# Rotary over two token tiles, padded GLA queries copied by ScalarE, and the second layer's convolution norm in borrowed memory

## The chip, the cores and the metric

The kernel runs on one core of one Trainium2 chip. A core has TensorE (PE in the profile, with its weight loads as PEld), VectorE (DVE), ScalarE (ACT), GpSimd (POOL) and SyncE (SP), which issues the DMAs. Each engine works through its own list of instructions in order, and waits on semaphores for the others. The metric is the device time of one execution, in microseconds (us), and its median over several runs.

## The reference: what is computed

Two layers of a mixer for a diffusion generator, in float32: 1024 latent tokens and 256 context tokens of width 1024. Each layer projects the normalised input once, and feeds three branches; a gate multiplies each branch, and one output projection joins them.

```python
pl = _project(hl, w_in); pc = _project(hc, w_in)        # hc: the context's h; layer 1 needs only k, v and decay of it
# A: convolution of width 31 over the tokens, then a norm over the 256 channels, then silu
u = conv(a_val * sigmoid(a_glu)) + conv_b
u = ((u - mean(u)) * rsqrt(var(u) + eps) * ln_w + ln_b);  a = silu(u) * silu(a_gate)
# B: windowed attention; q (8 heads) and k (2 heads) of 64 get a rotary on the latent tokens
rot = concat([-x[..., 32:], x[..., :32]]);  x = x * cos + rot * sin
# C: bidirectional gated linear attention (GLA), 4 heads, dk 32, dv 64, chunks of 64 tokens
q_in = q * exp(b);  k_in = k * exp(-b)                  # b: cumulative log decay in a chunk
att = where(causal, q_in @ k_in, 0);  o = att @ v + q_in @ S
S = decay * S + (k * exp(b_last - b)) @ v               # the state, from chunk to chunk
```

## The kernel before, in words

Tokens are columns in some stages and rows in others, in tiles of 128: ten tiles, 0 and 1 being the context. h lies transposed in three chunks: c=0 (context, 256 tokens, tile `HC`, 4096 columns), c=1 and c=2 (512 latent tokens each, tiles `H1`, `H2`). A float32 product is made of three passes over high and low parts (`three`, line 673), so PE's bulk is `ps<-WS,H` (weights stationary), or `ps<-H,WS` (tokens stationary).

The order of the instructions is made by a planner. Each piece of work is a generator (a lane) with a priority; `loop` (line 201) goes on with the ready lane of the best priority, where ready is judged by clocks of the engines that `Model` (line 49) keeps from a cost formula. The lists it writes are then fixed. Every instruction is recorded through a helper (line 43), so that all rows of the profile show L43; one goes by tiles. `SM` are 14 small slots of 512 columns, `WR` slots for raw weights and for scratch, `ps` the banks of PSUM, `mix` the wide tiles in which the branches' values stand.

`phase_a` (line 1571) runs a layer's input projection group by group, in the order of `GROUPS` (line 1735): convolution input (0, 1), GLA's v (10), GLA's q and k (8), attention's k and v (5), its q (3, 4), the convolution's gate (2), GLA's gate (9), attention's gates (6, 7). PE fills a PSUM bank by 48 or 96 matmuls, ACT copies it out (`SM<-ps 128x512`), and the bank is free again. Beside these groups run lanes:

- `ev_qk_b` (line 898) takes a pair of token tiles of groups 5, 3 or 4: ACT copies the bank to an `SM` slot, POOL applies `rope` (line 886) to each of the two tiles of a latent pair, and a DMA stores the pair. A pair of k and v has 2 heads of k to turn, a pair of q 4 heads. There are 8 pairs of k and v and 16 of q in both layers.
- `gla_states` (line 1059), one lane for each direction d: DVE forms b_last - b, ACT its exp, POOL multiplies by k (`SM<-SM,mix`), PE transposes the product (`ps<-idr,SM`) and multiplies it by v, DVE steps the state S. POOL's list holds these products between the rotaries.
- `gla_out` (line 1121), one call for each of 10 token tiles in layer 0 and 8 in layer 1, two lanes in parallel: ACT makes exp(b/16) and exp(-b/16) of both directions, the products with q and k follow, PE multiplies the two (`ps<-SM,SM 128*64 128x256`, the score matmuls), DVE applies the causal mask, PE sums, and a norm follows. q goes into `qx`, padded tiles in which head h of the 128 rows has its own block and zeros elsewhere, hence four products of 32x128.
- `conv_taps` (line 924): 62 DVE instructions a layer (`mix<-U,small,mix`, 128x1295 or 128x1024), placed wherever the planner finds DVE free for 0.3 us.
- `conv_ln` (line 939), the norm over channels of a chunk: PE transposes, DVE statistics, PE transposes back, ACT and DVE finish. It takes `SM` slots. In layer 1 one lane does c=1 and then c=2.
- `attn_start` (line 1186) opens the attention. It uses `HC`'s memory for its keys' and queries' tiles, which the flag `hcfree1` guards in layer 1.

Of the kernel before, what the change touches and what calls it, by code (L numbers as in the profile page):

```python
# [164 lines left out]
class Hybrid:  # L165
# [124 lines left out]
    def mix_new(self, dt):  # L290

        t, old = self.tile("mix4", 4 * TC, dt), self.mixes[1]
        m, b = self.nc.part(t)
        m[1, b] = self.nc.touched(old) if old is not None else 0.0
        self.mixes[1] = t
        return t

    def mix(self, a, t, p=slice(None)):
# [584 lines left out]
                self.flag(f"v{l}.{i}")  # L883
        return ev

    def rope(self, x, nh, blk, tmp):

        nc = self.nc
        x4 = x.rearrange("p (h a b) -> p h a b", a=2, b=32)
        t4 = tmp.rearrange("p (h a b) -> p h a b", a=2, b=32)  # L890
        cos, sin = [self.rt[:, s * 256 + blk * 32:s * 256 + blk * 32 + 32][:, None, None, :].to_broadcast([128, nh, 2, 32]) for s in range(2)]
        e = nc.gpsimd
        e.tensor_tensor(t4, x4[:, :, ::-1, :], sin, op=ALU.mult)
        e.tensor_tensor(x4, x4, cos, op=ALU.mult)
        e.tensor_tensor(x4[:, :, 0], x4[:, :, 0], t4[:, :, 0], op=ALU.subtract)
        e.tensor_tensor(x4[:, :, 1], x4[:, :, 1], t4[:, :, 1], op=ALU.add)

    def ev_qk_b(self, l, name, dst, nh):

        def ev(i0, p):  # L900
            nc = self.nc
            yield self.need("SM"), self.need("WR", 1, 1), f"rope{l}"
            s, tmp = self.sm(512), self.get("WR")
            s3 = s.rearrange("p (s c) -> p s c", s=2)
            nc.scalar.activation(s3, p, ACTF.Copy)
            yield
            if i0 >= 2:
                for r in range(2):
                    self.rope(s3[:, r, 0:nh * 64], nh, i0 + r - 2, tmp[:, r * 256:r * 256 + nh * 64])
            self.free(tmp)  # L910
            yield
            nc.sync.dma_start(dst[i0:i0 + 2].rearrange("s p c -> p s c"), s3)
            self.free(s)
            for i in (i0, i0 + 1):
                self.flag(f"{name}{l}.{i}")
        return ev
# [19 lines left out]
                    nc.vector.scalar_tensor_tensor(acc, src, self.p_conv_w(l, j, s), acc, op0=ALU.mult, op1=ALU.add)  # L936
        self.flag(f"conv{l}")

    def conv_ln(self, l, c):
        nc = self.nc  # L940
        t0, n = CH[c]
        nt = n // 128
        yield self.need("SM", (nt + 1) // 2, 2)
        xs = [self.sm(512).rearrange("p (q x) -> p q x", q=2) for _ in range((nt + 1) // 2)]
        for q0 in range(0, nt, 2):
            yield self.bank_need("tr")
            tp = self.bank_get("tr")
            for q in (q0, q0 + 1):
                o = col(t0) + q * 128
                for j in range(2):  # L950
                    nc.tensor.transpose(tp[:, (q - q0) * 256 + j * 128:(q - q0) * 256 + (j + 1) * 128],
                                        self.mix(j, slice(o, o + 128)), self.idf)
            yield
            mv = self.ti(4).rearrange("p (q x) -> p q x", q=2)
            for r in range(2):
                bs = self.bst[:, q0 + r]
                nc.vector.bn_stats(bs, tp[:, r * 256:(r + 1) * 256])
                nc.vector.bn_aggr(mv[:, r], bs)
            rs = self.rstd(mv[:, :, 1], 1.0, 2)
            yield  # L960
            for r in range(2):
                nc.vector.tensor_scalar(xs[q0 // 2][:, r], tp[:, r * 256:(r + 1) * 256], mv[:, r, 0:1], rs[:, r:r + 1],
                                        op0=ALU.subtract, op1=ALU.mult)
            self.free(tp)
        yield
        for j in range(2):
            yield self.bank_need("tr")
            bk = self.bank_get("tr")
            for q in range(nt):
                nc.tensor.transpose(bk[:, q * 128:(q + 1) * 128], xs[q // 2][:, q % 2, j * 128:(j + 1) * 128], self.idf)  # L970
            yield None, self.need("SM", 2), f"ag{l}.0.{c}", f"ag{l}.1.{c}"
            ys, ts = self.sm(512), self.sm(512)
# [9 lines left out]
            self.free(ys, ts)  # L982
        self.free(*xs)
        self.flag(f"ln{l}{c}")


# [134 lines left out]
    def gla_out(self, l, i, qx, v):  # L1121
        nc = self.nc
        o = col(i * 128)
        yield self.need("SM", 2), self.rest(v), f"T{l}.0.{self.hslot(i)[0]}"
        self.load_vz(i, v)
        ws, A = self.sm(512), self.sm(512)
        w = ws.rearrange("p (a t) -> p a t", a=4)
        for d in range(2):
            b = self.mix(4 + d, slice(o, o + 128))
            nc.scalar.activation(w[:, d], b, ACTF.Exp, scale=1.0 / 16.0)  # L1130
            nc.scalar.activation(w[:, 2 + d], b, ACTF.Exp, scale=-1.0 / 16.0)
        yield self.at(ws)
        for d in range(2):
            nc.gpsimd.tensor_tensor(w[:, 2 + d], w[:, 2 + d], self.mix(3, slice(o, o + 128)), op=ALU.mult)
            for h in range(4):
                r = slice(32 * h, 32 * h + 32)
                nc.vector.tensor_tensor(qx[d][r, h], w[r, d], self.mix(2, slice(o, o + 128), r), op=ALU.mult)
        yield None, self.bank_need("tr")
        at = self.bank_get("tr")
        for d in range(2):  # L1140
# [34 lines left out]
        tp = self.bank_get("tr")  # L1175
# [395 lines left out]
    def phase_a(self, l):  # L1571
# [9 lines left out]
        for g in GROUPS[:-1]:  # L1581
# [25 lines left out]
            elif g == 2:  # L1607
                yield from self.t_group(l, g, self.ev_agate(l), cx)

                def ln():  # L1610
                    for c in range(1 if l else 0, 3):
                        yield from self.conv_ln(l, c)
                self.go(ln(), 3)
            elif g == 9:
                yield from self.t_group(l, g, self.ev_mgate(l, 6), cx)
            else:
                self.cap.update(mm=2, tr=CAPB[0], ac=CAPB[1])
                self.cap["md"] = 0 if l else MDC
# [216 lines left out]
```

## Time and profile before

| | |
|---|---|
| median of 3 runs | 1350.08 us (1346.76 to 1352.33) |
| the profiled execution | 1350.69 us, its span 1348.9 us |
| mean granted TensorE clock | 0.977 |
| PE / DVE / ACT / POOL busy | 1253.7 / 962.9 / 560.2 / 542.9 us |
| instructions of PE / DVE / ACT / POOL | 9198 / 1856 / 1251 / 769 |

Layer 0's projection groups from the convolution's input to GLA's gate lie before 330 us, those of layer 1 between about 790 and 1068 us, the attentions behind them. A row of a timeline shows the start, the duration, the engine, the operation with its tiles and shapes, how many alike were joined (x), and in brackets the idle time ahead of it with what ended it.

### The profile page before, as it was taken

How to read it: one execution, taken by the hardware profiler on the slowest of the kernel's cores; microseconds unless marked ns; L12 is line 12 of the kernel's file. 1: busy time of each engine (PE TensorE's matmuls, PEld its weight loads, DVE VectorE, ACT ScalarE, POOL GpSimd, SP SyncE). 2: the span in 40 equal slices, each digit the busy share in tenths (PEclk: the TensorE clock that was granted, in tenths of full speed). 3: DMA queues.
4: the chain of work that ended last, by engine and by line, in shares of the span. 5: the costliest groups of instructions: out<-in, count | busy, mean ns of one | idle time of the engine just before them, and what ended most of it. 6: DMA issues, size and time to landing. Idle time of an engine off the chain costs nothing. (4 is left out here: it accounts for less than half of the span.)

```text
span 1348.9 us, 24464 instructions
## 1 busy us (share of the span) xinstructions
PE 1253.7 (93%) x9198; PEld 1089.8 (81%) x9198; DVE 962.9 (71%) x1856; ACT 560.2 (42%) x1251; POOL 542.9 (40%) x769
## 2 busy tenths in 40 slices
PE   5999997889999999899999889988899999999997
PEld 3678886778788777779988879977787888898997
DVE  5835894888556577777776676896966478887864
ACT  3711431112223456456652461341112256676751
POOL 1410065956223334434341132056792335645430
PEclk9999988999999999899999989989999999999999
DMA  9453113222114333432113441113232113311112
GB/s 328 143 151 102 47 32 99 59 73 74 29 32 126 120 102 106 137 106 67 48 40 110 139 168 56 53 40 104 69 81 54 39 43 102 98 44 52 63 36 79
DMA packets 113239, 116.48 MB, mean 86 GB/s; under 512 B 38464, under 2 KB 81760, under 8 KB 113120
## 3 DMA queue, kind: packets, MB, share of 16 engines
q1 hardware_dynamic: 113120, 114.92, 28.2%
q8 instruction: 72, 1.18, 0.4%
q14 instruction: 47, 0.39, 0.1%
HBM read 95.47 MB, written 19.42 MB: 85 GB/s over the span
## 5 line engine op out<-in xcount | busy, mean ns | idle before, releaser
L43 PE MATMUL ps<-H,WS 128*128 128x512 f32 x1344 | 339.1, 399 | 3.6 <-ACT U L43 1.7
L43 PEld LDWEIGHTS ps<-H,WS 128*128 128x128 f32 x1344 | 245.1, 189 | 64.2 <-issue 10.0
L43 PE MATMUL ps<-WS,H 128*128 128x256 f32 x1704 | 258.3, 294 | 8.1 <-DVE H L43 4.7
L43 ACT ACTIVATE SM<-ps 128x512 f32<-128x512 f32 (+3 forms) x180 | 92.6, 517 | 397.8 <-PE ps L43 284.2
L43 PEld LDWEIGHTS ps<-WS,H 128*128 128x128 f32 x1704 | 232.1, 198 | 21.4 <-issue 10.2
L43 PE MATMUL ps<-idr,SM 128*128 128x128 f32 (+1 forms) x1076 | 150.5, 273 | 38.1 <-POOL SM L43 25.5
L43 DVE SCALAR_TENSOR_TENSOR mix<-U,small,mix 128x1295 f32<-128x1295 f32 (+1 forms) x120 | 177.6, 1526 | 0.2
L43 PEld LDWEIGHTS ps<-idr,SM 128*128 128x128 f32 (+1 forms) x1076 | 124.1, 143 | 62.2 <-POOL SM L43 29.6
L43 DVE SCALAR_TENSOR_TENSOR H<-ps,H 128x512 fp32r<-128x512 f32 x160 | 105.7, 681 | 46.3 <-ACT H L43 46.1
L43 ACT ACTIVATE SM<-SM,stat 128x641 f32<-128x641 f32 (+2 forms) x144 | 110.5, 769 | 56.4 <-DVE stat L43 43.0
L43 ACT ACTIVATE H<-ps 128x512 fp32r<-128x512 f32 x176 | 99.4, 597 | 80.5 <-PE ps L43 73.9
L43 POOL TENSOR_TENSOR SM<-SM,SM 128x256 f32<-128x256 f32 (+4 forms) x91 | 72.8, 808 | 149.0 <-ACT SM L43 112.5
L43 POOL TENSOR_TENSOR tir<-tir,mhalf 128x1 f32<-128x1 f32 (+2 forms) x55 | 44.9, 820 | 197.8 <-DVE tir L43 173.4
L43 DVE CUSTOM_DVE_ANT_0 SM<-ps,SM,small 128x640 f32<-128x640 f32 (+2 forms) x128 | 102.3, 809 | 25.5 <-PE ps L43 24.7
L43 POOL TENSOR_TENSOR SM<-SM,WR 128x128 f32<-128x128 f32 (+2 forms) x117 | 90.8, 793 | 21.4 <-DVE SM L43 14.2
L43 PE MATMUL ps<-H,H 128*128 128x256 f32 x552 | 97.5, 286 | 0.0
L43 PE MATMUL ps<-H 128*128 128x512 f32 x320 | 97.0, 409 | 0.2 <-DVE H L43 0.2
L43 PE MATMUL ps<-SM,SM 128*32 128x128 f32 (+4 forms) x764 | 81.3, 295 | 12.5 <-DVE SM L43 7.8
L43 PEld LDWEIGHTS ps<-H,H 128*128 128x128 f32 x552 | 81.6, 189 | 1.4 <-issue 0.4
L43 POOL TENSOR_SCALAR SM<-SM,tir 128x640 f32<-128x640 f32 (+2 forms) x77 | 67.7, 892 | 28.5 <-DVE tir L43 18.0
L43 PE MATMUL ps<-WS,SM 128*128 128x256 f32 x248 | 70.2, 283 | 0.0
L43 PE MATMUL ps<-H,SM 128*128 128x256 f32 x248 | 69.4, 280 | 0.0
(150 smaller groups left out, 2121.9 us busy)
## 6 DMA issues: line engine op xcount, KB each, us to landing
WR<-in_w_in_dram SPq DMA_DIRECT2D x80, 256.0 KB, 3.9
WR<-in_w_mod_dram SPq DMA_DIRECT2D x64, 256.0 KB, 3.1
WR<-in_w_out_dram SPq DMA_DIRECT2D x32, 256.0 KB, 3.4
SM<-vd SPq DMA_DIRECT2D x116, 64.0 KB, 2.4
x<-SM SPq DMA_DIRECT2D x20, 256.0 KB, 2.3
SM<-x SPq DMA_DIRECT2D x20, 256.0 KB, 4.3
qd<-SM SPq DMA_DIRECT2D x18, 256.0 KB, 2.2
mix<-in_x_dram SPq DMA_DIRECT2D x8, 512.0 KB, 8.3
```

Source lines behind the costliest of these rows:

```text
L43: r = getattr(self._e, op)(*a, **k)
```

## The change

1. `rope` takes both token tiles of a pair at once, in five POOL instructions instead of two times four: the sine products of either half (two), the cosine product over everything, the subtraction and the addition.
2. `gla_out`: ACT's four exps of 128x128 become two of 128x256; the products with q and with k are two DVE instructions of 128x256 (before: eight of 32x128 on DVE, two of 128x128 on POOL); eight new ACT copies of 32x128 then carry q into the padded `qx`.
3. Layer 1's `conv_ln` works in the memory of `HC` (the context's h, which is no longer needed by then), as two lanes of priority 3, one for a chunk; `hcfree1` is given at their end, and `attn_start` of layer 1 waits for it.

```diff
-    def rope(self, x, nh, blk, tmp):
...
-        e.tensor_tensor(t4, x4[:, :, ::-1, :], sin, op=ALU.mult)
-        e.tensor_tensor(x4, x4, cos, op=ALU.mult)
-        e.tensor_tensor(x4[:, :, 0], x4[:, :, 0], t4[:, :, 0], op=ALU.subtract)
-        e.tensor_tensor(x4[:, :, 1], x4[:, :, 1], t4[:, :, 1], op=ALU.add)
+    def rope(self, x, t, nh, blk):
...
+        for a in range(2):
+            e.tensor_tensor(t5[:, :, :, a], x5[:, :, :, 1 - a], sin.to_broadcast([128, 2, nh, 32]), op=ALU.mult)
+        x4 = x.rearrange("p s (g b) -> p s g b", b=32)
+        e.tensor_tensor(x4, x4, cos.to_broadcast([128, 2, 2 * nh, 32]), op=ALU.mult)
+        for a, op in ((0, ALU.subtract), (1, ALU.add)):
+            e.tensor_tensor(x5[:, :, :, a], x5[:, :, :, a], t5[:, :, :, a], op=op)
...
-    def conv_ln(self, l, c):
+    def conv_ln(self, l, c, own=None):
...
+            xs = [own[:, 512 * q:512 * q + 512] for q in range(2)]
+            yield self.rest(own)
...
+        both = self.mix(slice(4, 6), slice(o, o + 128))
+        for a in range(2):
+            nc.scalar.activation(w[:, 2 * a:2 * a + 2], both, ACTF.Exp, scale=(1.0 - 2 * a) / 16.0)
+        yield self.at(ws)
+        for a in range(2):
+            nc.vector.tensor_tensor(w[:, 2 * a:2 * a + 2], w[:, 2 * a:2 * a + 2],
+                                    self.mix(2 + a, slice(o, o + 128))[:, None, :].to_broadcast([128, 2, 128]), op=ALU.mult)
+        yield
         for d in range(2):
-            b = self.mix(4 + d, slice(o, o + 128))
-            nc.scalar.activation(w[:, d], b, ACTF.Exp, scale=1.0 / 16.0)
-            nc.scalar.activation(w[:, 2 + d], b, ACTF.Exp, scale=-1.0 / 16.0)
-        yield self.at(ws)
-        for d in range(2):
-            nc.gpsimd.tensor_tensor(w[:, 2 + d], w[:, 2 + d], self.mix(3, slice(o, o + 128)), op=ALU.mult)
             for h in range(4):
                 r = slice(32 * h, 32 * h + 32)
-                nc.vector.tensor_tensor(qx[d][r, h], w[r, d], self.mix(2, slice(o, o + 128), r), op=ALU.mult)
+                nc.scalar.activation(qx[d][r, h], w[r, d], ACTF.Copy)
...
+        if l:
+            yield f"hcfree{l}"
...
+                def ln1():
+                    hc = self.hc_new(F32)
+                    yield tuple([self.go(self.conv_ln(l, c, hc[:, (c - 1) * 2048:c * 2048]), LNP) for c in (1, 2)])
+                    self.hc_new(F32R)
+                    self.flag(f"hcfree{l}")
+                self.go(ln1() if l else ln(), LNP if l else 3)
...
-                if l:
-                    self.flag(f"hcfree{l}")
```

POOL's list in layer 0, at the second pair of k and v, before the change. `SM2_271` holds the pair, `SM14` the cosines and sines, `WR0_272` the scratch; `SM8_266` and `SM5_268` are the products with k for the states of chunk 1, both directions:

```order
L43 TENSOR_TENSOR WR0_272_1795<-SM2_271_1794,SM14_1_65 128x128
L43 TENSOR_TENSOR SM2_271_1794<-SM2_271_1794,SM14_1_65 128x128
L43 TENSOR_TENSOR SM2_271_1794<-SM2_271_1794,WR0_272_1795 128x2x32 x2
L43 TENSOR_TENSOR WR0_272_1795<-SM2_271_1794,SM14_1_65 128x128
L43 TENSOR_TENSOR SM2_271_1794<-SM2_271_1794,SM14_1_65 128x128
L43 TENSOR_TENSOR SM2_271_1794<-SM2_271_1794,WR0_272_1795 128x2x32 x2
L43 TENSOR_TENSOR SM8_266_1758<-SM8_266_1758,mix_64 128x512
L43 TENSOR_TENSOR SM5_268_1766<-SM5_268_1766,mix_64 128x512
```

The same place of POOL's list after the change:

```order
L43 TENSOR_TENSOR SM8_266_1738<-SM8_266_1738,mix_64 128x512
L43 TENSOR_TENSOR WR0_272_1794<-SM2_271_1793,SM14_1_65 128x2x2x32 x2
L43 TENSOR_TENSOR SM2_271_1793<-SM2_271_1793,SM14_1_65 128x2x128
L43 TENSOR_TENSOR SM2_271_1793<-SM2_271_1793,WR0_272_1794 128x2x2x32 x2
L43 TENSOR_TENSOR SM5_268_1763<-SM5_268_1763,mix_64 128x512
```

The first product moved ahead of the second pair's rotary, the second one is behind it as before, and the rotary has five instructions instead of eight. In the same way both products of chunk 2 (`SM8_276`, `SM5_281`) now stand ahead of the first rotary of q, where before the second of them stood behind it.

PE's list at the same place, before: the transposes of the two products, among the matmuls of attention's k and v on the context's and the latent tokens (`WS1_191`):

```order
L43 MATMUL ps0_66<-WS1_191_1029,H2_0_104_491 128x256 x12
L43 MATMUL ps0_66<-WS1_191_1029,H2_1_105_492 128x256 x12
L43 MATMUL ps0_66<-WS1_191_1029,H2_0_104_491 128x256 x12
L43 MATMUL ps0_66<-WS1_191_1029,H2_1_105_492 128x256 x12
L43 MATMUL ps1_67<-WS1_191_1029,H2_0_104_491 128x256 x12
L43 MATMUL ps2_68<-idr_81,SM8_266_1758 128x128 x4
L43 MATMUL ps1_67<-WS1_191_1029,H2_1_105_492 128x256 x12
L43 MATMUL ps3_69<-idr_81,SM5_268_1766 128x128 x4
```

And after:

```order
L43 MATMUL ps0_66<-WS1_191_1029,H2_0_104_491 128x256 x12
L43 MATMUL ps2_68<-idr_81,SM8_266_1738 128x128 x4
L43 MATMUL ps0_66<-WS1_191_1029,H2_1_105_492 128x256 x12
L43 MATMUL ps3_69<-SM10_182_1013,SM3_267_1739 32x128 x4
L43 MATMUL ps0_66<-WS1_191_1029,H2_0_104_491 128x256 x12
L43 MATMUL ps3_69<-SM11_183_1014,SM3_267_1739 32x128 x4
L43 MATMUL ps0_66<-WS1_191_1029,H2_1_105_492 128x256 x12
L43 MATMUL ps4_70<-idr_81,SM5_268_1763 128x128 x4
```

The first transposes moved ahead by 48 matmuls, and the second ones by 24 (of the 128x256 kind).

ACT's list at the first two calls of `gla_out` in layer 0, before (`SM3_309` and `SM2_311` hold their exps, `mix4` the decay):

```order
L43 ACTIVATE SM5_302_2310<-ps0_66 128x512
L43 ACTIVATE SM6_305_2403<-ps3_69 128x512
L43 ACTIVATE SM3_309_2428<-mix4_222_1355 128x128 x4
L43 ACTIVATE SM2_311_2458<-mix4_222_1355 128x128 x4
L43 ACTIVATE SM8_310_2429<-ps3_69 128x256
L43 ACTIVATE SM6_322_2602<-ps1_67 128x512
```

And after, where `SM12` to `SM1` are the padded queries:

```order
L43 ACTIVATE SM5_302_2320<-ps1_67 128x512
L43 ACTIVATE SM3_306_2330<-mix4_222_1355 128x256 x2
L43 ACTIVATE SM6_308_2351<-mix4_222_1355 128x256 x2
L43 ACTIVATE SM12_244_1554<-SM3_306_2330 32x128 x4
L43 ACTIVATE SM9_245_1555<-SM3_306_2330 32x128 x4
L43 ACTIVATE SM0_246_1556<-SM6_308_2351 32x128 x4
L43 ACTIVATE SM1_247_1557<-SM6_308_2351 32x128 x4
L43 ACTIVATE SM5_311_2423<-ps0_66 128x512
L43 ACTIVATE SM2_307_2331<-ps4_70 128x256
```

Sixteen copies that wait for DVE's products now stand between the exps and the next copy of a filled bank, `SM5_311<-ps0_66`.

More of the change, by code (lines that the diff above doesn't have):

```diff
@@ L295, in mix_new, with hc_new @@
         self.mixes[1] = t
+        return t
+    def hc_new(self, dt):
+        t, old = self.tile("HC", 4096, dt), self.HC
+        m, b = self.nc.part(t)
+        m[1, b] = self.nc.touched(old)
+        self.HC = t
         return t
@@ L884, in ev_v @@
         return ev
-    def rope(self, x, nh, blk, tmp):
[L888 to L892, printed above, removed]
-        e.tensor_tensor(t4, x4[:, :, ::-1, :], sin, op=ALU.mult)
-        e.tensor_tensor(x4, x4, cos, op=ALU.mult)
-        e.tensor_tensor(x4[:, :, 0], x4[:, :, 0], t4[:, :, 0], op=ALU.subtract)
-        e.tensor_tensor(x4[:, :, 1], x4[:, :, 1], t4[:, :, 1], op=ALU.add)
+    def rope(self, x, t, nh, blk):
+        e = self.nc.gpsimd
+        cos, sin = [self.rt[:, s * 256 + blk * 32:s * 256 + blk * 32 + 64].rearrange("p (r b) -> p r b", b=32)[:, :, None, :] for s in range(2)]
+        x5, t5 = [z.rearrange("p s (h a b) -> p s h a b", a=2, b=32) for z in (x, t)]
+        for a in range(2):
[4 more added lines that the diff above has]
+            e.tensor_tensor(x5[:, :, :, a], x5[:, :, :, a], t5[:, :, :, a], op=op)
     def ev_qk_b(self, l, name, dst, nh):
@@ L907, in ev @@
             if i0 >= 2:
-                for r in range(2):
-                    self.rope(s3[:, r, 0:nh * 64], nh, i0 + r - 2, tmp[:, r * 256:r * 256 + nh * 64])
+                self.rope(s3[:, :, 0:nh * 64], tmp.rearrange("p (s c) -> p s c", s=2)[:, :, 0:nh * 64], nh, i0 - 2)
             self.free(tmp)
@@ L942, in conv_ln @@
         nt = n // 128
-        yield self.need("SM", (nt + 1) // 2, 2)
-        xs = [self.sm(512).rearrange("p (q x) -> p q x", q=2) for _ in range((nt + 1) // 2)]
+        if own is None:
+            yield self.need("SM", (nt + 1) // 2, 2)
+            xs = [self.sm(512) for _ in range((nt + 1) // 2)]
+        else:
+            xs = [own[:, 512 * q:512 * q + 512] for q in range(2)]
+            yield self.rest(own)
+        x3 = [x.rearrange("p (q x) -> p q x", q=2) for x in xs]
         for q0 in range(0, nt, 2):
@@ L961, in conv_ln @@
             for r in range(2):
-                nc.vector.tensor_scalar(xs[q0 // 2][:, r], tp[:, r * 256:(r + 1) * 256], mv[:, r, 0:1], rs[:, r:r + 1],
+                nc.vector.tensor_scalar(x3[q0 // 2][:, r], tp[:, r * 256:(r + 1) * 256], mv[:, r, 0:1], rs[:, r:r + 1],
                                         op0=ALU.subtract, op1=ALU.mult)
@@ L969, in conv_ln @@
             for q in range(nt):
-                nc.tensor.transpose(bk[:, q * 128:(q + 1) * 128], xs[q // 2][:, q % 2, j * 128:(j + 1) * 128], self.idf)
-            yield None, self.need("SM", 2), f"ag{l}.0.{c}", f"ag{l}.1.{c}"
-            ys, ts = self.sm(512), self.sm(512)
+                nc.tensor.transpose(bk[:, q * 128:(q + 1) * 128], x3[q // 2][:, q % 2, j * 128:(j + 1) * 128], self.idf)
+            yield None, (self.need("SM", 2) if own is None else 0.0), f"ag{l}.0.{c}", f"ag{l}.1.{c}"
+            ys, ts = (self.sm(512), self.sm(512)) if own is None else (own[:, 1024:1536], own[:, 1536:2048])
             y, t = ys[:, 0:n], ts[:, 0:n]
@@ L981, in conv_ln @@
                                            op0=ALU.mult, op1=ALU.mult)
-            self.free(ys, ts)
-        self.free(*xs)
+            if own is None:
+                self.free(ys, ts)
+        if own is None:
+            self.free(*xs)
         self.flag(f"ln{l}{c}")
@@ L1610, in ln @@
                 def ln():
-                    for c in range(1 if l else 0, 3):
+                    for c in range(3):
                         yield from self.conv_ln(l, c)
-                self.go(ln(), 3)
+                def ln1():
[4 more added lines that the diff above has]
+                self.go(ln1() if l else ln(), LNP if l else 3)
             elif g == 9:
@@ L1626, in phase_a @@
                         self.flag("mods")
-                    if p == 7:
+                    if p == 7 and (c or l == 0):
                         self.flag({0: f"hcfree{l}", 1: f"h1out{l}", 2: f"h2out{l}"}[c])
@@ L1732, in run @@
             self.loop(self.go(self.program(), 9))
+LNP = 3
 GROUPS = [0, 1, 10, 8, 5, 3, 4, 2, 9, 6, 7]
```

## The prediction

> **What bounds the kernel now.** I read the page's first part, then the waits of PE, the busy time by stretches, and at last the timelines of PE and POOL around PE's longest idle times. PE's busy time and the list of what it waited for (us in total, times, longest):
>
> ```profile
> PE 1253.7 (93%) x9198; PEld 1089.8 (81%) x9198; DVE 962.9 (71%) x1856; ACT 560.2 (42%) x1251; POOL 542.9 (40%) x769
> ```
>
> ```profile
> PE ps L43 <- POOL SM L43: 26.4, 14, 8.7
> PE ps L43 <- DVE SM L43: 15.2, 16, 2.0
> ```
>
> PE works 1253.7 of 1348.9 us, so the 95 us in which it stands still are nearly all there is to gain while its matmuls stay the same. The first two kinds of wait, 26.4 and 15.2 us, are those that the rotary's and GLA's edits can reach. Where they lie, by stretches (PE, PEld, DVE, ACT, POOL, granted clock):
>
> ```profile
> 178.00:330.00 152.00, 129.80 (x1188) 116.36 (x1187) 117.44 (x168) 28.19 (x77) 103.49 (x126) 0.91 0.26 68
> 330.00:500.00 170.00, 168.41 (x1188) 137.28 (x1188) 104.56 (x249) 62.49 (x141) 53.66 (x86) 1.00 0.28 83
> 880.00:1000.00 120.00, 107.33 (x969) 97.24 (x969) 97.33 (x139) 28.66 (x64) 83.31 (x106) 0.97 0.26 70
> 1068.00:1120.00 52.00, 50.41 (x287) 42.18 (x286) 40.91 (x101) 27.17 (x59) 22.17 (x41) 1.00 0.23 62
> ```
>
> Layer 0's GLA and rotary stage (178 to 330) leaves PE idle for 22.2 us and its clock at 0.91; layer 1's (880 to 1000) for 12.7 us. Right behind layer 0's stage PE is busy for 168.4 of 170 us: nothing there swallows time that is won earlier, so a gain in the stage reaches the end. The waits one by one, as PE's rows show them:
>
> ```profile
> 212.52 1.12 PE L43 MATMUL ps<-idr,SM 128*128 128x128 f32 x4 [8.68 <-POOL SM L43]
> ...
> 250.87 0.66 PE L43 MATMUL ps<-idr,SM 128*128 128x128 f32 x4 [4.09 <-POOL SM L43]
> ...
> 252.62 2.73 PE L43 MATMUL ps<-WS,H 128*128 128x256 f32 x12
> ...
> 255.63 1.69 PE L43 MATMUL ps<-WS,H 128*128 128x256 f32 x12
> ...
> 278.18 0.33 PE L43 MATMUL ps<-SM,SM 128*64 128x64 f32 x2 [0.95 <-DVE SM L43]
> ...
> 298.82 0.65 PE L43 MATMUL ps<-SM,SM 128*64 128x256 f32 x4 [1.87 <-DVE SM L43]
> 301.35 1.12 PE L43 MATMUL ps<-SM,SM 128*64 128x256 f32 x4 [1.87 <-DVE SM L43]
> 302.40 2.93 PE L43 MATMUL ps<-WS,H 128*128 128x256 f32 x12
> ...
> 918.30 0.66 PE L43 MATMUL ps<-idr,SM 128*128 128x128 f32 x4 [2.96 <-POOL SM L43]
> ```
>
> **The rotary in front of GLA's states.** The 8.68 us come about in POOL's list: the second pair of k and v is turned, and only then come the products with k that PE transposes.
>
> ```profile
> 197.49 1.27 POOL L43 TENSOR_TENSOR WR<-SM,SM 128x128 f32<-128x128 f32 x1 [4.49 <-ACT SM L43]
> 198.84 1.60 POOL L43 TENSOR_TENSOR SM<-SM,SM 128x128 f32<-128x128 f32 x1
> 200.52 3.02 POOL L43 TENSOR_TENSOR SM<-SM,WR 128x64 f32<-128x64 f32 x2
> ...
> 209.94 3.75 POOL L43 TENSOR_TENSOR SM<-SM,mix 128x512 f32<-128x512 f32 x2
> 213.66 0.45 POOL L43 TENSOR_TENSOR WR<-SM,SM 128x128 f32<-128x128 f32 x1
> ...
> 214.72 0.60 POOL L43 TENSOR_TENSOR SM<-SM,WR 128x64 f32<-128x64 f32 x2
> ...
> 236.26 1.29 POOL L43 TENSOR_TENSOR SM<-SM,mix 128x512 f32<-128x512 f32 x1
> ...
> 243.08 1.89 POOL L43 TENSOR_TENSOR SM<-SM,SM 128x256 f32<-128x256 f32 x1
> ...
> 248.29 2.52 POOL L43 TENSOR_TENSOR SM<-SM,mix 128x512 f32<-128x512 f32 x1
> ```
>
> ```profile
> 195.40 15.94 DVE L43 SCALAR_TENSOR_TENSOR mix<-U,small,mix 128x1295 f32<-128x1295 f32 x10
> ```
>
> From 197.49 to 209.94 the eight instructions take 12.45 us, about 1.6 us each; the same shapes take 0.3 to 0.45 us from 213.66 on, after DVE's ten taps of 1.6 us have ended (195.40 + 15.94). Beside the taps POOL gets through about one instruction a tap, whatever its size. So it is the count that costs: five instead of eight. I take four of 1.6 us, and 2.0 for the longer cosine product (256 elements beside taps: 1.9 in the row 243.08), 8.4 us, so the rotary ends at 205.9.
>
> The first product leaves this queue altogether: its exp is done when POOL falls idle for the 4.49 us ahead of 197.49,
>
> ```profile
> 193.59 0.63 ACT L43 ACTIVATE SM<-SM 128x512 f32<-128x512 f32 x1 [7.03 <-DVE SM L43]
> ```
>
> so it runs from 194.3 to at most 196.9 (2.52 us beside taps, row 248.29). PE's transposes of it stand 48 matmuls earlier; at 1.69 us for 12 (row 255.63) that is 6.8 us before 203.84, where PE's wait began, or 197.1: no wait. The second product ends at 205.9 + 2.5 = 208.4; PE comes to it at about 203.0 (36 matmuls and three short groups after 197.1). It waits 5.4 us there, in place of 8.68: **-3.3 us**. If the taps are thinner there, the product runs in 1.29 and the rotary in 6, and 7 of the 8.68 go; if the queue is as slow as before, nothing goes.
>
> The 4.09 us before 250.87 come from the same pattern, the first rotary of q (the row 243.08 is part of it) between the first product of chunk 2 at 236.26 and the second at 248.29.
>
> Both products now stand ahead of the q rotaries, so the second would run behind the first, from 237.6, far before 246.78, where this wait began: **-4.1 us**. What is late next is the state chain itself, since PE's transposes moved forward too; I count that under the new waits. Behind this gap, and behind the pair of 1.87 us gaps, the clock was halved:
>
> ```profile
> 299.50:306.20 6.70, 4.85 (x25) 3.90 (x26) 6.57 (x11) 0.00 (x0) 1.47 (x3) 0.50 0.20 59
> ```
>
> Behind 250.87 twelve matmuls took 2.73 us instead of 1.69: **-1.0 us**. Behind 299.5, 4.85 us of work ran at clock 0.50, and half of it is **-2.4 us**. The stretch behind the 8.68 us keeps its halved clock in my sum, since 5.4 us remain.
>
> The Trainium skill, page "TensorE: Matmul & The Clock Gate", section "Part 1", lets the clock fall only after an idle window of about 3.4 us. No gap as long stood before 299.5, where the trace has 0.50; by that rule the 2.4 us wouldn't hang on these gaps, and the gain would be 2.4 us less. The trace decides.
>
> **The queries by ScalarE.** What DVE does for one `gla_out` now, and what ACT's 128x128 exps and DVE's 128x256 products cost:
>
> ```profile
> 290.01 4.52 DVE L43 TENSOR_TENSOR SM<-SM,mix 32x128 f32<-32x128 f32 x8
> ...
> 296.05 5.15 DVE L43 TENSOR_TENSOR SM<-SM,mix 32x128 f32<-32x128 f32 x8
> ...
> 277.70 0.43 DVE L43 TENSOR_TENSOR SM<-SM 128x256 f32<-128x256 f32 x1
> ...
> 287.06 0.91 ACT L43 ACTIVATE SM<-mix 128x128 f32<-128x128 f32 x4
> ```
>
> Before, PE waits for eight products, 4.5 to 5.2 us. After, for two products of 0.43 and eight copies; four exps of 128 elements take 0.91, so a copy of 128 about 0.23 and eight 1.8: 2.7 us in all, 1.8 to 2.5 us less than before. That covers both gaps of 1.87: **-3.7 us**. The 0.95 at 278.18 is the mask's step behind taps, and stays. ACT pays eight copies, 1.8 us, less two exps, about 0.3, for each of 18 tiles: some 27 us on an engine that is busy for 28 of 152 us in the stage; not on the path. Bounds: the copies could cost what a bank's copy of 512 costs, 0.6 each, 4.8 us in all, and then both gaps stay.
>
> The Trainium skill speaks against the move: "ScalarE: Activation LUTs", section "Rules for kernel authors", budgets about 0.3 us an ACTIVATE plus 0.83 ns an element. That would be an estimated 3.2 us for eight copies, and the gain would be about 2 us less. The row above has less, 0.23 each in a series.
>
> **Layer 1.** The wait of 2.96 stands behind the same kind of rotary:
>
> ```profile
> 908.93 0.70 POOL L43 TENSOR_TENSOR WR<-SM,SM 128x128 f32<-128x128 f32 x1 [2.71 <-ACT SM L43]
> ...
> 916.99 1.26 POOL L43 TENSOR_TENSOR SM<-SM,mix 128x512 f32<-128x512 f32 x1
> ```
>
> Eight instructions in 8.06 us; five of them would be 5.0 us by count: 3.0 us off, I take **-2.5**. GLA's outputs there wait in two short gaps:
>
> ```profile
> 967.44 1.82 PE L43 MATMUL ps<-SM,SM 128*64 128x256 f32 x12 [0.92 <-POOL SM L43]
> 969.95 0.65 PE L43 MATMUL ps<-SM,SM 128*64 128x256 f32 x4 [0.70 <-DVE SM L43]
> ```
>
> **-1.6 us** if both go. The norm of the convolution lies in 1068 to 1120, where PE idles for 1.6 of 52 us: moving its DVE and ACT work out of the attention's start can win 1.6 at most, I take **-0.5**. Its transposes cost PE the same wherever they stand. Its DVE and ACT work moves beside GLA's gate group, under whose matmuls it hides: they fill PE for 67.6 of 68 us.
>
> ```profile
> 1000.00:1068.00 68.00, 67.58 (x531) 53.53 (x530) 37.79 (x93) 16.06 (x49) 25.48 (x35) 1.00 0.22 55
> ```
>
> **New waits.** The planner put PE's transposes and score matmuls earlier by 24 to 84 matmuls (3 to 12 us), as if the engines kept its times, which POOL beside taps does not. Estimate: three waits of about 1 us, as the 0.95 and 0.92 above, **+3.0**; bounds 0 and 8.7 (the longest wait comes back whole).
>
> **Sum:** -3.3 - 4.1 - 1.0 - 2.4 - 3.7 - 2.5 - 1.6 - 0.5 + 3.0 = -16.1. From the profiled 1350.7, which is 0.6 above the median, that makes **1334.6 us**. All bounds at their good end: 3.7 more on the first rotary, 2.4 of its halved clock, 3.0 without new waits, 1.1 on the norm, 0.5 on layer 1: 1323.9.
>
> **Rivals.**
> 1. *More than the sum.* The first wait goes nearly whole and no new ones come: 1324, with 1318 if the order also closes the small gaps elsewhere that the 95 us still contain. For it: taps thin out while the state chain waits. Chance 0.17.
> 2. *No change.* POOL's pace is set by taps and PE's list was moved forward by as much as POOL became faster; the waits come back under other names: 8.7 of new waits in place of 3.0, the gaps before GLA's outputs (3.7 and 1.6) and the halved clock behind them (2.4). Sum -16.1 + 5.7 + 5.3 + 2.4 = -2.7: 1348. For it: the planner's clock is PE's and it fills to the edge. Against it: two of the gaps are waits behind whole rotaries that no longer stand there. Chance 0.17.
> 3. *Slower, by ACT's queue.* The copies wait for DVE's products, which stand behind taps of 1.6 us, and behind the copies ACT's next bank copy waits, without which PE gets no bank. A bank takes PE 5.92 us to fill:
>
> ```profile
> 264.55 5.92 PE L43 MATMUL ps<-WS,HC 128*128 128x256 f32 x48
> ```
>
> With two banks the copy may be late by that. It is only lost when DVE has more than about three taps ahead of the products (3 x 1.6 + 0.9 + 1.8 = 7.5 for one tile, 3.6 more for the second tile of a pair). If each of nine pairs of tiles lost 1.5 us, and 1.2 of clock behind it, that is +24.3, and 1334.6 becomes 1358.9. Against it: between the products at 290.01 and at 296.05 there was room for one tap alone, and ACT is idle four fifths of the stage. Chance 0.09. The wait of `attn_start` for the norm is no rival of its own: the norm starts a whole group, 68 us by the row above, ahead of it.
>
> **How the numbers follow.** Chances: forecast 0.57, rivals 0.17, 0.17 and 0.09. The range 1319 to 1350 covers the forecast, most of rival 1 and rival 2. A measurement of this kernel tells 0.5% (6.8 us) from no change: faster is below 1343.9, slower above 1357.5. Faster: 0.56 of the forecast, rival 1, and 0.02 of rival 2, together 0.75. Same: the rest of the forecast and of rival 2, 0.16. Slower: rival 3, 0.09.
>
> **What would show it.** Right: in POOL's timeline near 197 to 206 five rotary instructions of about 1.6 us; PE's wait for the first product gone, and one of about 5 us for the second; no wait of 4 us before q's first pair; clock 1.00 where the scores of layer 0's outputs stand; POOL's waits at PE down from 26.4 to under 15 us, DVE's by 5. Wrong: PE waiting for ACT's `SM` or for banks in 250 to 330 and 960 to 1000; a stage 178 to 330 that is as long as before; or an idle stretch at the start of layer 1's attention.

## The result, and the profile after

The changed kernel takes 1332.84 us (median; 1331.86 to 1335.86), beside 1348.42 us for the kernel before on the same chip (1345.08 to 1352.33): a ratio of 0.9887, 95% interval 0.9854 to 0.9921. Measured again later it took 1333.13, ratio 0.9895 (0.9866 to 0.9925). The forecast was 1334.6. The profiled execution took 1333.29 us, with a span of 1331.4.

Page and waits of the changed kernel: busy time of the engines, and what PE waited for (us in total, times, longest).

```profile
PE 1249.0 (94%) x9198; PEld 1087.5 (82%) x9198; DVE 941.9 (71%) x1766; ACT 601.2 (45%) x1356; POOL 485.2 (36%) x646
```

```profile
PE ps L43 <- POOL SM L43: 18.7, 11, 4.3
...
PE ps L43 <- ACT SM L43: 9.5, 10, 4.2
PE ps L43 <- DVE SM L43: 8.9, 8, 2.3
```

POOL has 123 instructions and 58 us less, ACT 41 us more. PE's waits for POOL fell from 26.4 to 18.7 us, those for DVE's `SM` from 15.2 to 8.9. PE has the same 9198 matmuls, so the two traces can be laid side by side by counting them. Up to each of the following places every kernel of the study has run the same matmuls: from the 1022nd to the 3394th (178.0 to 500.1 us before: layer 0's GLA stage and what follows it), to the 5855th (880.0: to the start of layer 1's GLA), and to the last one. In the profiled executions:

| us between these matmuls | layer 0, 178 to 500 | 500 to 880 | layer 1, from 880 |
|---|---|---|---|
| before | 322.1 | 379.9 | 460.7 |
| changed | 305.6 | 375.3 | 465.3 |
| changed, measured again | 304.0 | 374.3 | 463.9 |

Layer 0's stage won 16.5 to 18 us, more than forecast; the middle won 5; layer 1, for which I had 4.6 us less, needed 3 to 5 us more.

The rows that answer to those of the prediction, first PE's. The first is the transposes of the first product, without a wait; the second those of the second product; the fifth is the mask's step of the first outputs. The last two answer to the scores of a later output and to layer 1's wait of 2.96.

```profile
195.04 0.60 PE L43 MATMUL ps<-idr,SM 128*128 128x128 f32 x4
...
205.33 1.11 PE L43 MATMUL ps<-idr,SM 128*128 128x128 f32 x4 [4.30 <-POOL SM L43]
...
228.30 0.65 PE L43 MATMUL ps<-idr,SM 128*128 128x128 f32 x4
...
251.06 1.20 PE L43 MATMUL ps<-SM,SM 128*64 128x256 f32 x8
...
257.42 0.33 PE L43 MATMUL ps<-SM,SM 128*64 128x64 f32 x2 [2.30 <-DVE SM L43]
...
276.71 0.65 PE L43 MATMUL ps<-SM,SM 128*64 128x256 f32 x4 [0.59 <-ACT SM L43]
...
895.46 0.66 PE L43 MATMUL ps<-idr,SM 128*128 128x128 f32 x4 [2.88 <-POOL SM L43]
```

The 8.68 us have become 4.30, the 4.09 before the second product of chunk 2 (now at 228.30) are gone, and so are the gaps before the scores (251.06). The mask's wait has grown from 0.95 to 2.30, PE waits twice for the new copies (0.59 at 276.71 and again at 317.36), and layer 1's 2.96 is still 2.88. POOL's second pair of k and v, and DVE's taps beside it:

```profile
192.16 1.29 POOL L43 TENSOR_TENSOR SM<-SM,mix 128x512 f32<-128x512 f32 x1 [2.17 <-ACT SM L43]
195.23 2.24 POOL L43 TENSOR_TENSOR WR<-SM,SM 128x128 f32<-128x128 f32 x2 [1.78 <-ACT SM L43]
197.55 1.88 POOL L43 TENSOR_TENSOR SM<-SM,SM 128x256 f32<-128x256 f32 x1
199.50 3.28 POOL L43 TENSOR_TENSOR SM<-SM,WR 128x128 f32<-128x128 f32 x2
202.75 2.52 POOL L43 TENSOR_TENSOR SM<-SM,mix 128x512 f32<-128x512 f32 x1
```

```profile
193.92 10.23 DVE L43 SCALAR_TENSOR_TENSOR mix<-U,small,mix 128x1295 f32<-128x1295 f32 x6
```

Five instructions in 7.5 us, from 195.23 to 202.75 (forecast 8.4), and the second product ends at 205.27. DVE's list has six taps there, where it had ten. In layer 1, before 895.46, the same five instructions need 7.0 us and the product behind them 2.24, since DVE has taps up to the end of it:

```profile
886.17 2.56 POOL L43 TENSOR_TENSOR WR<-SM,SM 128x128 f32<-128x128 f32 x2 [2.09 <-ACT SM L43]
...
893.17 2.24 POOL L43 TENSOR_TENSOR SM<-SM,mix 128x512 f32<-128x512 f32 x1
```

```profile
884.55 11.94 DVE L43 SCALAR_TENSOR_TENSOR mix<-U,small,mix 128x1024 f32<-128x1024 f32 x8
```

The new chain before the scores, two tiles at once, on DVE and ACT:

```profile
248.00 4.14 DVE L43 TENSOR_TENSOR SM<-SM,mix 128x256 f32<-128x256 f32 x4
```

```profile
249.00 5.14 ACT L43 ACTIVATE SM<-SM 32x128 f32<-32x128 f32 x16 [1.70 <-DVE SM L43]
...
289.98 2.54 ACT L43 ACTIVATE SM<-SM 32x128 f32<-32x128 f32 x8
```

A product of 128x256 took 1.03 us beside POOL's rotary (the mean of these four), not 0.43, and a copy 0.32 (2.54 for eight). That lies between my 0.23 and an estimated 0.41 by the budget on the page "ScalarE: Activation LUTs" of the Trainium skill ("Rules for kernel authors"); the page gives that budget for an ACTIVATE whose bias is a pointer operand, and these copies are given no bias. And a wait that the kernel before does not have, in layer 1's attention:

```profile
1253.01 0.90 PE L43 MATMUL ps<-idr,SM 128*128 128x128 f32 x3 [3.00 <-POOL SM L43]
```

From 1251.9 on the clock was at 0.50 for 6.8 us. The execution measured again has the wait too (2.98), with 3.4 us at 0.50.

### The profile page after: what moved, and what is told of

Same layout as the page of the kernel before. It is cut to its first block, busy times and chain, and to the rows that moved or that the text cites. A ratio compares the mean times of both kernels' runs of the same rounds, so it can differ in the third digit from the quotient of the medians.

```text
span 1331.4 us, 24334 instructions
## 1 busy us (share of the span) xinstructions
PE 1249.0 (94%) x9198; PEld 1087.5 (82%) x9198; DVE 941.9 (71%) x1766; ACT 601.2 (45%) x1356; POOL 485.2 (36%) x646
## 5 line engine op out<-in xcount | busy, mean ns | idle before, releaser
L43 PEld LDWEIGHTS ps<-WS,H 128*128 128x128 f32 x1704 | 229.3, 195 | 23.2 <-issue 10.4
L43 PE MATMUL ps<-idr,SM 128*128 128x128 f32 (+1 forms) x1060 | 149.1, 274 | 31.3 <-POOL SM L43 18.7
L43 POOL TENSOR_TENSOR tir<-tir,mhalf 128x1 f32<-128x1 f32 (+2 forms) x55 | 49.6, 905 | 183.4 <-DVE tir L43 158.6
L43 POOL TENSOR_TENSOR SM<-SM,SM 128x512 f32<-128x512 f32 (+3 forms) x53 | 53.0, 1009 | 128.3 <-ACT SM L43 108.1
L43 ACT ACTIVATE SM<-SM 32x128 f32<-32x128 f32 (+5 forms) x201 | 70.4, 360 | 39.0 <-DVE SM L43 32.2
L43 POOL TENSOR_TENSOR WR<-SM,SM 128x256 f32<-128x256 f32 (+1 forms) x48 | 48.7, 1035 | 67.1 <-ACT SM L43 57.1
```

Source lines behind the costliest of these rows:

```text
L43: r = getattr(self._e, op)(*a, **k)
```

## The experiments

Two theories stood against each other from the start. The first is the prediction's: POOL pays by the instruction beside DVE's taps, and DVE's chain before the scores is too long, so each part wins its own terms. The second: the planner's new order does it, and the parts only work together. All ratios are to the kernel before, run on the same chip in the same rounds.

| kernel | median us | ratio | 95% interval |
|---|---|---|---|
| rope_alone | 1359.93 | 1.0093 | 1.0058 to 1.0128 |
| gla_alone | 1353.23 | 1.0048 | 1.0025 to 1.0071 |
| ln_alone | 1357.49 | 1.0060 | 1.0038 to 1.0081 |
| rope_gla | 1328.24 | 0.9862 | 0.9835 to 0.9889 |
| new_in_old | 1335.52 | 0.9910 | 0.9881 to 0.9938 |
| old_in_new | 1359.40 | 1.0094 | 1.0071 to 1.0117 |
| taps_before | 1303.87 | 0.9681 | 0.9652 to 0.9709 |
| taps_after | 1311.48 | 0.9741 | 0.9716 to 0.9766 |
| rope_held | 1342.72 | 0.9953 | 0.9925 to 0.9980 |
| gla_held | 1351.43 | 1.0030 | 1.0007 to 1.0053 |
| taps_wait | 1339.22 | 0.9939 | 0.9912 to 0.9965 |
| after_again | 1333.13 | 0.9895 | 0.9866 to 0.9925 |

### Each part alone, planned anew

rope_alone is the kernel before with this hunk (and its call in `ev_qk_b`) only:

```diff
-    def rope(self, x, nh, blk, tmp):
+    def rope(self, x, t, nh, blk):
```

> The kernel before with the rotary's part alone. My theory (POOL pays by the instruction beside DVE's taps): layer 0's wait of 8.68 us falls to about 4.3 as in the changed kernel, the one of 4.09 goes with the slow clock behind it, layer 1's 2.96 shrinks by 0 to 2; the two gaps of 1.87 before GLA's scores stay. About 9 us faster, 1339. Rival (the gain comes from the planner's new order as a whole, and needs all parts): within 3 us of before, 1345 to 1351.

gla_alone has the hunk of `gla_out` only:

```diff
-                nc.vector.tensor_tensor(qx[d][r, h], w[r, d], self.mix(2, slice(o, o + 128), r), op=ALU.mult)
+                nc.scalar.activation(qx[d][r, h], w[r, d], ACTF.Copy)
```

> The kernel before with the part of gla_out alone. My theory: the waits of 8.68 and 4.09 us behind rotaries stay; the two gaps of 1.87 before layer 0's scores and the slow clock behind them go, and 1.6 us in layer 1: about 7 us faster, 1341. Rival (ACT's queue: the copies hold up the copies of PSUM's banks, and the rotary's gain hides it): no change or slower, 1348 to 1355, with PE waiting for banks in 250 to 330 us.

ln_alone has the hunks of `hc_new`, `conv_ln`, `attn_start` and `phase_a` only:

```diff
-    def conv_ln(self, l, c):
+    def conv_ln(self, l, c, own=None):
```

> The kernel before with layer 1's convolution norm alone in the context's h. My theory: -0.5 us, 1348, no measurable change, layer 0 as before. Rival (the earlier norm or the later release of that memory makes layer 1's attention longer, as the 5 us that the changed kernel loses again behind 1060 us suggest): 4 to 6 us slower, 1353.

rope_gla has the first two parts, and the norm as before:

```diff
-                self.go(ln1() if l else ln(), LNP if l else 3)
+                self.go(ln(), 3)
```

> The changed kernel with the norm as before. My theory: as the changed kernel within 2 us, 1333. Rival (the norm's part costs the 5 us behind 1060 us): 1328. Other rival (the norm's part gives the gain in layer 1): 1338 or more.

Each part alone is slower than before, by 0.5 to 0.9%, and two together are 1.4% faster. My theory failed in all four; in the last, 1328 is what the rival had said. In layer 0 its first step holds: with the rotary's part alone the 8.68 us become 4.17 and the 4.09 are gone. But of this gain 1.1 us are left at the end of layer 0's stage (the table below). The largest wait that takes it back begins at 308. PE's row, and DVE's rows of the same stretch:

```profile
313.77 0.47 PE L43 MATMUL ps<-SM,SM 128*64 128x64 f32 x2 [5.52 <-DVE SM L43]
```

```profile
298.31 5.66 DVE L43 TENSOR_TENSOR SM<-SM,mix 32x128 f32<-32x128 f32 x8
304.00 3.62 DVE L43 SCALAR_TENSOR_TENSOR mix<-U,small,mix 128x1295 f32<-128x1295 f32 x2
307.54 4.93 DVE L43 TENSOR_TENSOR SM<-SM,mix 32x128 f32<-32x128 f32 x8
312.49 0.77 DVE L43 COPY_PREDICATED SM<-gmask,ps 128x256 f32<-128x256 uint8 x2
```

PE waits 5.52 us for the mask of one tile, which stands in DVE's list behind the eight short products of its own tile, two taps, and the eight of the next tile: 14 us of work, beside q's rotaries. Eight products took 4.1 to 5.2 us before and up to 5.7 here; the mean of all 144 rose from 430 to 507 ns. So the rotary's part, alone, brings PE sooner to a wait on DVE. That `gla_out`'s part would have shortened it is read from the rows; in the changed kernel the longest wait of this kind in layer 0 is 2.30.

The three stretches of the table above tell where each kernel's time went:

| us between the same matmuls | layer 0, 178 to 500 | 500 to 880 | layer 1, from 880 |
|---|---|---|---|
| before | 322.1 | 379.9 | 460.7 |
| rope_alone | 321.0 | 373.3 | 475.7 |
| gla_alone | 313.7 | 374.9 | 473.5 |
| ln_alone | 322.5 | 378.9 | 466.9 |
| rope_gla | 305.8 | 375.8 | 459.1 |

What rope_alone loses lies in layer 1, 15.0 us. gla_alone wins 8.4 us in layer 0's stage (about 6 expected), and loses 12.8 in layer 1. PE's largest waits there are 3.47 us for DVE at 955, the mask's step of an output, and 3.75 at 1163 in the attention. At the 7461st matmul (1089.3 us before), up to which both kernels have run the same ones, gla_alone is only 0.4 us behind: the rest is lost in the attention, which none of its changed instructions touches. ln_alone leaves layer 0 alone and makes layer 1 6 us longer, as the rival had it. The first long wait that it adds, with DVE's rows beside it:

```profile
1078.75 1.42 PE L43 MATMUL ps<-H,WS 128*128 128x512 f32 x5 [3.29 <-DVE SM L43]
```

```profile
1075.83 2.26 DVE L43 TENSOR_TENSOR WS<-WR,WS 128x512 fp32r<-128x512 f32 x2 [0.23 <-ACT WS L43]
1078.02 1.27 DVE L43 SCALAR_TENSOR_TENSOR SM<-SM,ps 128x512 f32<-128x512 f32 x2
```

PE waits for a bank that DVE empties at 1078, and ahead of that in DVE's list stand two splits of the next weights. The norm's last DVE step (`mix<-HC,U`) had ended at 1070.4. rope_gla is the fastest complete kernel of the study: without the norm's part layer 1 takes 459.1 us instead of 465.3 or 463.9. Alone, that part costs 0.6%; on top of the other two 1333 against 1328, a difference that the two intervals (0.9835 to 0.9889 and 0.9866 to 0.9925) do not separate; the two were also measured on different chips, each beside the kernel before.

### Instructions and order, taken apart

What a part does through its instructions, and what through the planner's new order, was mixed so far. In these kernels the planner is charged with one set of instructions while the other is written out. PE's and SP's lists are then word for word those of the order that is charged. `issue` charges the planner, `_e` writes an instruction that it does not see. new_in_old writes the new rotary and `gla_out` in the order of before:

```diff
-        e.tensor_tensor(t4, x4[:, :, ::-1, :], sin, op=ALU.mult)
...
+        f = lambda *a, **k: self.nc.issue("pool", "tensor_tensor", a, k)
+        f(t4, x4[:, :, ::-1, :], sin, op=ALU.mult)
...
+        e = self.nc.gpsimd._e
...
+            e.tensor_tensor(t5[:, :, :, a], x5[:, :, :, 1 - a], sin.to_broadcast([128, 2, nh, 32]), op=ALU.mult)
```

> The new instructions of the rotary and of gla_out in the order of the kernel before: the planner is charged with the old instructions, so PE's and SP's lists are those of before word for word (norm as before). Theory 1 (the instructions do it: fewer on POOL beside the taps, a shorter chain before the scores): the 8.68 us falls to about 4.5, the 4.09 to under 1, the two 1.87 go with the slow clock behind: about 1336. Theory 2 (the new order does it, as the parts alone, which were 6 to 13 us slower, suggest): 1345 or more.

old_in_new is the reverse, made from the changed kernel:

```diff
-                nc.scalar.activation(qx[d][r, h], w[r, d], ACTF.Copy)
+                nc.issue("act", "activation", (qx[d][r, h], w[r, d], ACTF.Copy), {})
...
+                nc.vector._e.tensor_tensor(qx[d][r, h], w[r, d], self.mix(2, slice(o, o + 128), r), op=ALU.mult)
```

> The old instructions of the rotary and of gla_out in the order of the changed kernel: the planner is charged with the new ones (norm as in the changed kernel). Theory 1: 12 us or more slower than the changed kernel, 1345 to 1360, with waits for DVE before and behind the scores and for POOL before the states' transposes. Theory 2: within 5 us of the changed kernel, 1333 to 1338.

New instructions in the old order: 1335.52, as theory 1 had it (1336). Old instructions in the new order: 1359.40, slower than before. So the instructions carry the gain, the order does not: with the old instructions it costs 0.9%. (This order is that of all three parts, so the norm's share is in the 0.9%.) One step of theory 1 falls all the same. The two kernels' rows of PE at the second product, new_in_old first:

```profile
206.57 1.12 PE L43 MATMUL ps<-idr,SM 128*128 128x128 f32 x4 [4.86 <-POOL SM L43]
```

```profile
206.61 1.11 PE L43 MATMUL ps<-idr,SM 128*128 128x128 f32 x4 [4.29 <-POOL SM L43]
```

DVE's taps beside POOL's eight old instructions in old_in_new:

```profile
194.33 9.49 DVE L43 SCALAR_TENSOR_TENSOR mix<-U,small,mix 128x1295 f32<-128x1295 f32 x6
```

Each halves the 8.68 us by itself. In the new order eight old rotary instructions do as well as five new ones (4.29 against 4.30 us), since DVE has six taps there instead of ten, and POOL is free when they end. The instruction count matters where the taps go on. What the old instructions cost in the new order lies behind: 2.71 us before the first scores, 1.88 and 2.01 later, and 11 us in layer 1 (476.4 against 465.3).

rope_held and gla_held write one part each in the order of before, the new rotary being `rope2` there:

```diff
-        e.tensor_tensor(t4, x4[:, :, ::-1, :], sin, op=ALU.mult)
...
+        f = lambda *a, **k: self.nc.issue("pool", "tensor_tensor", a, k)
+        f(t4, x4[:, :, ::-1, :], sin, op=ALU.mult)
...
+                self.rope2(s3[:, :, 0:nh * 64], tmp.rearrange("p (s c) -> p s c", s=2)[:, :, 0:nh * 64], nh, i0 - 2)
```

> The rotary's new instructions alone, with PE's, DVE's, ACT's and SP's lists word for word those of before. If the parts add up as my sum has them: the 8.68 us to about 4.9 and the 4.09 to under 1 as with both parts in this order, layer 1's 2.96 to 2.4; about 8 us faster, 1340. If DVE's short products pay for POOL's longer instructions, as where the rotary's part was planned alone: the gaps before the scores grow from 1.87 to 3 us or more, and 1345 or above.

```diff
+            nc.vector._e.tensor_tensor(w[:, 2 * a:2 * a + 2], w[:, 2 * a:2 * a + 2],
+                                       self.mix(2 + a, slice(o, o + 128))[:, None, :].to_broadcast([128, 2, 128]), op=ALU.mult)
...
+                nc.scalar._e.activation(qx[d][r, h], w[r, d], ACTF.Copy)
```

> The new instructions of gla_out alone, with PE's and SP's lists word for word those of before. If the parts add up: the two gaps of 1.87 and the slow clock behind them go, 1.6 us in layer 1, the waits of 8.68 and 4.09 stay: about 6 us faster, 1342, and with the rotary's alone together the 12 that both gave in this order. If the eight copies in ACT's list hold up the banks: no change, 1347.

The parts don't add up even in one order: -0.47% and +0.30% alone, -0.90% together. It shows in layer 0's stage, 178 to 500: 322.1 us before, 316.3 in rope_held, 322.7 in gla_held, 311.5 with both (new_in_old). PE's waits in rope_held, then in gla_held, show why:

```profile
210.79 1.12 PE L43 MATMUL ps<-idr,SM 128*128 128x128 f32 x4 [4.80 <-POOL SM L43]
...
295.33 1.12 PE L43 MATMUL ps<-SM,SM 128*64 128x256 f32 x4 [2.93 <-DVE SM L43]
```

```profile
210.90 1.11 PE L43 MATMUL ps<-idr,SM 128*128 128x128 f32 x4 [8.58 <-POOL SM L43]
...
249.27 1.11 PE L43 MATMUL ps<-idr,SM 128*128 128x128 f32 x4 [4.07 <-POOL SM L43]
...
334.12 0.65 PE L43 MATMUL ps<-SM,SM 128*64 128x256 f32 x4 [1.66 <-ACT SM L1147]
```

With the rotary alone the two gaps of 1.87 before the scores become 2.93 and 0.56, and others come: PE's waits for DVE's `SM` between 178 and 360 us add up to 9.1 us, before to 5.9. DVE's products became only a little longer, 443 ns on the mean of 144 instead of 430; PE comes to them sooner. With `gla_out` alone the two waits on POOL stay, the gaps before the scores are gone, and PE waits for the new copies instead (L1147; 4.9 us in eight times). The profiled execution of gla_held took 1344.70, the 12 timed ones 1344.70 to 1355.77 with a median of 1351.43: why most are slower than the profiled one I can't say.

### Without the taps

Both kernels, planned alike, write out only the first of each 31 taps:

```diff
-                    nc.vector.scalar_tensor_tensor(acc, src, self.p_conv_w(l, j, s), acc, op0=ALU.mult, op1=ALU.add)
+                    nc.issue("dve", "scalar_tensor_tensor", (acc, src, self.p_conv_w(l, j, s), acc), {})
```

> The kernel before, planned alike, without 120 of the 124 convolution taps: the convolution's sum is left out but for its first tap, the planner is charged with all. If POOL pays by the instruction only beside the taps, the second rotary of k and v takes about 3.3 us instead of 12.45 and the waits of 8.68 and 4.09 us nearly vanish: about 1327. If a rotary instruction costs the same without taps: 1343 or more.

> The changed kernel, planned alike, without 120 of the 124 taps, as above. If the gain hangs on the taps, little of the 15 us between the two kernels is left: within 5 us of the kernel before without taps, about 1324. If the gain is the order's or the chain's own: 10 us or more below the kernel before without taps.

The kernel before loses 44 us with its taps, the changed one 21: without them the change makes the kernel 7.6 us slower (1311.48 against 1303.87). By stretches, layer 0's stage takes 292.5 us without taps before and 290.8 changed, so that of the 16.5 us won there 1.7 are left: this gain hangs on the taps. Layer 1 takes 445.6 and 453.1, so the loss lies there, and it is not the taps that make it. The second pair of k and v in taps_before:

```profile
191.14 0.46 POOL L43 TENSOR_TENSOR WR<-SM,SM 128x128 f32<-128x128 f32 x1 [4.88 <-ACT SM L43]
191.68 0.46 POOL L43 TENSOR_TENSOR SM<-SM,SM 128x128 f32<-128x128 f32 x1
192.22 0.60 POOL L43 TENSOR_TENSOR SM<-SM,WR 128x64 f32<-128x64 f32 x2
...
194.43 2.55 POOL L43 TENSOR_TENSOR SM<-SM,mix 128x512 f32<-128x512 f32 x2
```

Eight instructions in 3.3 us (191.14 to 194.43) instead of 12.45, and PE waits for neither product. This is what the Trainium skill, page "SBUF — State Buffer", section "SBUF: two separate sides", says of the port that VectorE and GpSimd share: whoever starts first holds it for a whole instruction. The rows agree: a 64-element instruction of POOL took 1.5 us beside a tap of 1.6, and 0.3 without.

A last kernel has rope_gla's parts, and a planner that places a tap only where POOL, too, is done:

```diff
-                yield self.idle("dve", 300)
+                yield lambda: max(self.nc.clock["dve"] - 300, self.nc.clock["pool"])
```

> The rotary's and gla_out's parts, the norm as before, and one new condition in the planner: a convolution tap may be placed only where POOL, too, has no work left by the planner's clock. If the contention of taps and POOL is what is left (without taps the kernel before loses 44 us): the waits of 4 and 2 us in layer 0's stage shrink, 1320 or less. If the taps, put off, then delay the norm or collide elsewhere: 1328 to 1340.

It is slower than rope_gla, 1339.22. The wait for the second product falls to 0.73 us, but the taps that were put off come later, eleven of them with little between from 333.8 to 353.4 us, the last three ahead of work that frees a bank (PE's row, then DVE's):

```profile
354.10 6.12 PE L43 MATMUL ps<-H,WS 128*128 128x512 f32 x14 [4.53 <-DVE U L43]
```

```profile
348.93 4.51 DVE L43 SCALAR_TENSOR_TENSOR mix<-U,small,mix 128x1295 f32<-128x1295 f32 x3
353.36 1.87 DVE L43 SCALAR_TENSOR_TENSOR U<-SM,ps 128x512 f32<-128x512 f32 x3
```

Layer 0's stage is 4.0 us longer than rope_gla's (309.8 against 305.8), layer 1 is 9.1 us longer (468.2 against 459.1).

after_again is the changed kernel unedited, beside the last three.

> The changed kernel beside the others on one chip, for a closer interval: if the norm's part costs as it did alone, it stays some 4 us above the version without it, 1332 to 1334 and a ratio to before of 0.989; if not, 1328 and 0.986.

It came out nearer to the first case, 0.9895 and 4.9 us above rope_gla's median, though the intervals overlap.

## Why the prediction was right, and where it wasn't

The time was right, 1334.6 against 1332.84, and the change is faster. That the sum is so near is luck: in the profiled executions layer 1 came out 9.2 us above its terms (4.6 lost instead of 4.6 won), and that was made up by 4.6 us in the middle, which the change did not make, and by layer 0, which won 16.5 us where the sum had 14.5, less the new waits.

- **The first wait.** Forecast 5.4 in place of 8.68, measured 4.30. The reason was half right: one rotary instruction a tap is borne out (taps_before), but in the new order six taps instead of ten shorten the wait as much by themselves (old_in_new), and I did not read that out of DVE's list.
- **The 4.09 us** went whole, as forecast.
- **The scores' gaps** went, and the mask's wait that I left alone at 0.95 became 2.30. The chain's cost was mis-sized: 0.43 a product and 0.23 a copy in the sum, 0.4 to 1.5 (0.79 on the mean of 36) and 0.31 in the trace.
- **The clock.** I had -1.0 and -2.4 for work at half clock. In layer 0's stage the clock was at 0.50 for 27.3 us before, for 13.6 us in the changed kernel and for 3.4 when it was measured again; PE was busy with the same matmuls for 298.3, 294.2 and 290.8 us. So the terms came, and somewhat larger.
- **New waits.** I had three of about 1 us. In layer 0 there are three: the mask's 2.30 in place of 0.95, and twice 0.59 for the copies. The longest new one, 3.00, is in layer 1's attention. With layer 1's 2.88 it keeps PE's waits for POOL at 18.7 us, where I had under 15.
- **The middle, 500 to 880 us:** 4.6 us less that I had not forecast and that are not the change's: rope_held, gla_held and new_in_old, whose PE lists are those of before, need 376.6, 373.0 and 374.1 us there. The clock was at 0.50 for 20.5 us of this stretch in the profiled execution of before, and for 10.2 in that of the changed kernel.
- **Layer 1** failed. I had -4.6 us; it is 3 to 5 us longer. The rotary's term of -2.5 was worth 0.1 (2.96 became 2.88): five instructions took 7.0 us instead of the 5.0 of my sum, and the product behind them 2.24 instead of 1.26, because the taps went on. Other waits went instead, so that at the 6734th matmul (988.8 us before; the kernels of the table have run the same ones up to it) the changed kernel has won 3.4 to 3.8 us of layer 1. The loss lies behind it, in the last of GLA's outputs, the gates and the attention:

| us of layer 1 | to the 6734th matmul | behind it |
|---|---|---|
| before | 108.8 | 351.9 |
| order of before: rope_held / gla_held / new_in_old | 105.8 / 108.4 / 107.3 | 352.3 / 352.6 / 352.8 |
| changed / measured again | 105.0 / 105.4 | 360.3 / 358.5 |
| rope_gla | 106.1 | 353.0 |
| rope_alone / ln_alone / old_in_new | 110.0 / 108.7 / 112.2 | 365.6 / 358.3 / 364.2 |
| without taps: before / changed | 94.7 / 94.0 | 350.9 / 359.1 |

- **The norm.** I had -0.5 for it. The kernels with it in a new order lose 6 to 12 us behind that place, with the taps or without; but rope_alone, which has no part of it, loses 14, and rope_gla only 1. So a new order alone can cost as much there, and what the norm's part costs by itself is not separated from it: no kernel with the norm's part in the order of before was run. Nor is it shown that the wait for `hcfree1` has no share.
- **Adding up.** The sum treated each part as worth its own terms. It isn't so: in the order of before, layer 0's stage wins 5.8 us by the rotary, loses 0.6 by `gla_out`, and wins 10.6 by both. Rival 2's picture of waits that come back under other names is what rope_alone does in layer 0, but in the changed kernel the other part is there to meet them. Of rival 3, ACT's queue, only the copies' own lateness shows: PE waits 4.9 us (gla_held), 6.6 us (new_in_old) and, in the changed kernel, 2.2 us (0.59 twice in layer 0, 0.64 and 0.39 in layer 1) for them.

## What to carry to other kernels

Here POOL got through about one instruction a tap of DVE (1.5 us for 64 elements, 2.5 for 512), and DVE's product of 128x256 took 0.42 us alone and up to 1.5 beside the rotary. Where two engines hold each other up like this, count the instructions on both sides, and try the two changes together: in one order they gave layer 0 10.6 us, alone 5.8 and -0.6. Where a planner writes the lists, time a change twice, planned anew and in the old order: layer 1 took 458 to 461 us in the four kernels with the order of before, and 459 to 476 in the six that were planned anew, a scatter as large as the gain. And look which third kind of work makes a wait dear: without the taps 1.7 of the 16.5 us that layer 0 won are left.

## What the runs showed of the hardware

- 120 taps on DVE cost 44 us of the kernel before (1347.95 with them, 1303.87 without), although DVE is busy for 71% of the span and PE for 93%.
- The clock fell to 0.5 behind waits of about 2 us: from 183.5 to 187.0 us behind one of 2.09 in the changed kernel, and from 258.6 to 262.1 behind the 2.30. In the execution profiled again, the same wait (2.08, from 183.5 to 185.6) left it at 1.00. So what a wait of this length costs differs between executions of one kernel.
- The clock reached 1.00 at 22.9 us in the profiled execution of before and at 32.5 in that of ln_alone, whose PE list is the same there; at the 1022nd matmul, 178.0 us before, PE was 3.6 us behind.
